# Whole fp32 products in place of three fp32r partial products in a hybrid DeltaNet and attention layer

## The chip, the cores and the metric

The kernel runs on one core of one Trainium2 chip. The metric is the device time of one execution in microseconds. All inputs, outputs and weights are fp32 in device memory.

## The reference

One layer of a diffusion backbone over 2048 latent tokens of width 1024, with 256 context tokens that go through the same weights and only serve as a prefix. A modulated RMS norm gives h; one wide projection of h feeds two token mixers; both are projected to 1024, merged by gates computed from h, projected once more and added to x:

```python
h = _rmsnorm(x, norm_w) * (1.0 + scale[:, None]) + shift[:, None]
...
qkv, beta_r, decay_r, kb, vb = _split_cols(h @ w_state, STATE_SIZES)
za, qb, zb, ga, gb = _split_cols(h @ w_rest, REST_SIZES)
qa, ka, va, g, bt = _gdn_inputs(qkv, beta_r, decay_r, conv_w, a_log, dt_bias)
oa, _, _ = _gdn_bidir(qa, ka, va, g, bt, s_f, s_b, True)
ya = _gdn_output(oa, za, gdn_norm_w)
...
yb = ob * jax.nn.silu(zb)
x = x + gate[:, None] * _merge(ya, yb, ga, gb, w_proj_a, w_proj_b, w_out)
...
def _merge(ya, yb, ga, gb, w_proj_a, w_proj_b, w_out):
    y = jax.nn.sigmoid(ga) * (ya @ w_proj_a) + jax.nn.sigmoid(gb) * (yb @ w_proj_b)
    return y @ w_out
```

The output of attention over window, context and sink is `ob`. The first mixer is a bidirectional gated DeltaNet in chunks of 64 with 4 heads of 128; the second is windowed attention with 8 query heads of 64 on 2 key heads.

## The kernel before

Tokens lie in five groups: gi 0 to 3 of 512 latent tokens, and group 4, the 256 context tokens. Widths are cut into blocks of 128, so a dense product is a loop over k of 8 (over 1024) or 4 (over 512) matmuls that sum up in one PSUM bank of 128 x 512.

**How a dense product is made.** TensorE has an fp32 matmul and a reduced one, fp32r. The kernel uses the reduced one with two parts for each operand: the high part is a copy rounded to fp32r, the low part the fp32 value less the high part. Each step over k is then three fp32r matmuls into the same bank: high by high, low by high, high by low (`fm_dense`, L586 to L588; `tm_dense`, L413 to L415; `project`, L1293 to L1295; `product`, L1556 to L1558). The parts are made by three engines: `make_h` writes h twice, `hh` and `hl`, of the transposed and normed x (ScalarE scales it into `h32`, GpSimd copies the high part, VectorE subtracts, L373 to L376); `weights` loads a column block of w_in into `wr` and splits it into `wh` and `wl` (L239 to L244).

**Stages**, in order of time:
1. Modulation (`mps`, L313): two rows per vector of shift and scale, then the columns `modA` and `modB`.
2. h and the state columns, two token blocks at a time: norm, transpose (`hps`, L371), h, and the 272 narrow columns of w_in (`tmps`, `tm_dense`), from which come the attention keys and values and the decay inputs.
3. q, k and v of the DeltaNet (`qkv`, `lps`): 12 column blocks over all groups, the short convolution on VectorE (L625), norms, transposes and spills to device memory; beside it the decays, and the attention queries (`q_pass`, 256 columns a time).
4. The gates (`gates`, `rest_run`, `rps`): 24 column blocks, first over groups 2 and 3, beside triangular inverses on VectorE (`base`, L809 and L811); then over groups 1 and 0, between the products of the scan.
5. The scan over chunks in both directions (`scan`: `ksps`, `vps`, `sps`, `aps`, `ops`, whole fp32 products of 128 x 128 for each head).
6. Attention (`scores`, `weighted`), with the rest of the gates and the projections of groups 1, 2 and 0 between (`project`, `pps`), let in a few at a time by `paced`.
7. The projections of group 3, and then the output.

**The output stage** multiplies the merged rows `ysp` by w_out, gated by columns. It cuts the 2048 rows into eight units of 256 and w_out into four quarters of 512 x 512 (`B11` to `B22`). Unit 0 takes the eight plain products of quarters; units 1 to 7 take Winograd's form of Strassen's scheme, seven products of quarters each, for which sums of quarters are made (`S1` to `S4` of the rows, `T1` to `T4` of w_out) and every one split into high and low parts. VectorE, ScalarE and GpSimd follow an order written by hand there (`manual_schedule`). The projections of group 3 put off their last two sums (`late_sum`) into that stage.

Elsewhere the order of the instructions on each engine comes from a scheduler that runs over the program with priorities (`high_priority`) and with waits that the program states (`issue_after`). Buffers come from pools; a tile that takes over another's place waits until that one is no longer read.

Of the kernel before, what the change touches and what calls it, by code (L numbers as in the profile page):

```python
# [7 lines left out]
F32 = mybir.dt.float32  # L8
# [32 lines left out]
def _hybrid(ctx, tc, nc, V, S, G, T, ins, out, dbg, upto):  # L41
# [73 lines left out]
    def hpool(name, groups):  # L115
# [9 lines left out]
    hh, hl = {}, {}  # L125
# [27 lines left out]
    def hsrc(c):  # L153

        if c < NCB:
            return hh[4][:, :, c * 128:c * 128 + 128], hl[4][:, :, c * 128:c * 128 + 128]
        b = c - NCB
        o = (b % 4) * 128
        return hh[b // 4][:, :, o:o + 128], hl[b // 4][:, :, o:o + 128]
# [73 lines left out]
    def weights(src, kt, by_act=False):  # L233

        wh = wq.tile([128, KT, 128], F32R, name="wh")
        wl = wq.tile([128, KT, 128], F32R, name="wl")
        for k in range(0, kt, 4):
            wr = wq.tile([128, 4, 128], F32, name="wr", bufs=2)
            dma(wr, src[k * 128:(k + 4) * 128].rearrange("(k p) c -> p k c", p=128))  # L239
            if by_act:  # L240
                S.copy(wh[:, k:k + 4], wr)
            else:
                G.tensor_scalar(wh[:, k:k + 4], wr, 1.0, 1.0, op0=ALU.mult, op1=ALU.mult)  # L243
            V.tensor_tensor(wl[:, k:k + 4], wr, f32(wh[:, k:k + 4]), op=ALU.subtract)  # L244
        return wh, wl
# [4 lines left out]
    if True:  # L250
# [113 lines left out]
        def make_h(xts, hi, lo, cc):  # L364
            n = len(xts) * 128
            for k in range(0, KT, 2):
                h32 = px.tile([128, 2, 256], F32, name="h32", bufs=2)
# [7 lines left out]
                hi_ = G.tensor_scalar(hi[:, k:k + 2], h32[:, :, :n], 1.0, 1.0, op0=ALU.mult, op1=ALU.mult)  # L375
                lo_ = V.tensor_tensor(lo[:, k:k + 2], h32[:, :, :n], f32(hi[:, k:k + 2]), op=ALU.subtract)  # L376
                if k == 2:
                    made = [h, lo_]
# [1303 lines left out]
```

## Time and profile before

| | |
|---|---|
| time, median of 3 runs | 1964.41 us (1963.11 to 1968.98) |
| the profiled execution's own time | 1973.82 us |
| its span | 1972.1 us |
| instructions | 32045 |
| TensorE busy | 1910.1 us, 97% |
| VectorE, ScalarE, GpSimd busy | 1477.4, 815.9 and 657.4 us |
| granted clock of TensorE, mean | 0.991 |

In the profile PE is TensorE's matmuls and PEld its weight loads, DVE is VectorE, ACT ScalarE, POOL GpSimd and SP the engine whose queue issues most transfers; L586 is line 586 of the kernel. A group of instructions has its line, engine, operation, the names of output and inputs, the tile's size, a count, and then busy us and mean ns of one, and the idle time of the engine ahead of it with what ended that. Matmuls are pipelined: the duration of one reaches into the next, so the time that one takes up is read from the distance between two starts. In the timeline a row stands for one or several instructions of a kind (x2): start, length of all, engine, line, names.

### The profile page before, as it was taken

The numbers are of one execution on the slowest core, as the hardware profiler recorded it, in microseconds if no ns is written. First come the engines' busy times: TensorE is split into PE (matmuls) and PEld (weight loads), VectorE is DVE, ScalarE is ACT, GpSimd is POOL, SyncE is SP. The second block draws the span as 40 slices with busy tenths as digits, with TensorE's granted clock in tenths as the row PEclk, the third lists the DMA queues.
The fourth block names the chain that finished last, engine by engine and source line by source line (L and its number), as shares of the span: only waits on it lengthen the run. The fifth ranks groups of instructions, "written<-read, shape, count | busy, mean of one in ns | idle before, by whom it ended". The sixth has DMA issues, their size and how long they took to land. (4 is left out here: it accounts for less than half of the span.)

```text
span 1972.1 us, 32045 instructions
## 1 busy us (share of the span) xinstructions
PE 1910.1 (97%) x10943; PEld 1606.0 (81%) x10943; DVE 1477.4 (75%) x2853; ACT 815.9 (41%) x2008; POOL 657.4 (33%) x750
## 2 busy tenths in 40 slices
PE   6899999989999999999999999999999999999999
PEld 3888888778998787887888888888878887878787
DVE  7889766677776999999778767544787777757864
ACT  6865545554444322211122233324675555532321
POOL 2652111235543201104222334422555444430353
PEclk9999999999999999999999999999999999999999
DMA  7553226765546633537887777755555555448362
GB/s 267 162 154 94 86 89 160 188 163 168 155 149 162 188 106 115 152 93 211 226 243 224 225 217 228 205 157 183 173 164 168 172 164 171 137 120 283 123 224 86
DMA packets 385463, 333.12 MB, mean 169 GB/s; under 512 B 83800, under 2 KB 307344, under 8 KB 384660
## 3 DMA queue, kind: packets, MB, share of 16 engines
q1 hardware_dynamic: 366292, 295.40, 51.7%
q10 hardware_dynamic: 19008, 35.67, 4.9%
q8 instruction: 87, 1.43, 0.3%
q14 instruction: 76, 0.62, 0.1%
HBM read 220.28 MB, written 109.13 MB: 167 GB/s over the span
## 5 line engine op out<-in xcount | busy, mean ns | idle before, releaser
L586 PE MATMUL rps<-hh,wh 128*128 128x512 f32 x768 | 309.8, 403 | 4.3 <-DVE rt L880 3.2
L587 PE MATMUL rps<-hl,wh 128*128 128x512 f32 x768 | 308.3, 401 | 0.0
L588 PE MATMUL rps<-hh,wl 128*128 128x512 f32 x768 | 307.2, 400 | 0.0
L625 DVE SCALAR_TENSOR_TENSOR cacc<-y,cw,cacc 128x512 f32<-128x512 f32 (+1 forms) x224 | 165.0, 758 | 21.1 <-ACT cacc L623 18.8
L586 PEld LDWEIGHTS rps<-hh,wh 128*128 128x128 f32 x768 | 145.4, 189 | 39.8 <-DVE rt L880 3.7
L588 PE MATMUL lps<-hh,wl 128*128 128x512 f32 (+1 forms) x448 | 171.7, 383 | 1.2 <-DVE wl L244 1.2
L586 PE MATMUL lps<-hh,wh 128*128 128x512 f32 (+1 forms) x448 | 172.0, 384 | 0.8 <-POOL wh L243 0.6
L588 PEld LDWEIGHTS rps<-hh,wl 128*128 128x128 f32 x768 | 145.3, 189 | 32.7
L587 PEld LDWEIGHTS rps<-hl,wh 128*128 128x128 f32 x768 | 145.7, 190 | 31.8
L587 PE MATMUL lps<-hl,wh 128*128 128x512 f32 (+1 forms) x448 | 171.0, 382 | 0.0
L1006 DVE TENSOR_TENSOR pl<-pt,ph 128x512 fp32r<-128x512 f32 x156 | 105.5, 685 | 45.8 <-ACT ph L1004 44.9
L1004 ACT CAST ph<-pt 128x512 fp32r<-128x512 f32 x156 | 90.6, 585 | 110.7 <-PE pt L1002 72.1
L878 ACT ACTIVATE rt<-rps 128x512 f32<-128x512 f32 x96 | 57.2, 596 | 185.1 <-PE rps L588 168.2
L978 DVE CUSTOM_DVE_ANT_0 pr<-sc,band,sk 128x640 f32<-128x640 f32 (+1 forms) x128 | 106.7, 862 | 19.9 <-PE sc L974 12.7
L811 DVE TENSOR_TENSOR N<-N,btmp 128x62 f32<-128x62 f32 (+30 forms) x124 | 118.1, 953 | 3.0
L988 POOL TENSOR_SCALAR pr<-pr,sm 128x640 f32<-128x640 f32 (+1 forms) x128 | 101.0, 809 | 55.8 <-DVE sm L986 40.3
L809 DVE TENSOR_TENSOR btmp<-N 128x62 f32<-128x62 f32 (+30 forms) x124 | 115.8, 934 | 3.1
L980 ACT ACTIVATE pr<-pr,sm 128x640 f32<-128x640 f32 (+1 forms) x128 | 104.0, 815 | 24.6 <-DVE sm L978 20.9
L244 DVE TENSOR_TENSOR wl<-wr,wh 128x512 fp32r<-128x512 f32 x120 | 90.8, 768 | 24.1 <-POOL wh L243 21.2
L1293 PE MATMUL pps<-yh,wph 128*128 128x512 f32 x256 | 105.7, 415 | 2.1 <-DVE tb L1304 2.0
L243 POOL TENSOR_SCALAR wh<-wr 128x512 fp32r<-128x512 f32 x72 | 50.3, 711 | 159.4 <-PE lps L587 57.2
L1295 PE MATMUL pps<-yh,wpl 128*128 128x512 f32 x256 | 101.9, 399 | 1.2 <-POOL wpl L1255 1.2
(396 smaller groups left out, 4961.4 us busy)
## 6 DMA issues: line engine op xcount, KB each, us to landing
wr<-in_w_in_dram SPq DMA_DIRECT2D x120, 256.0 KB
kw<-Ksp SPq DMA_DIRECT2D x28, 384.0 KB
x<-vsp SPq DMA_DIRECT2D x36, 256.0 KB
k<-ksp SPq DMA_DIRECT2D x34, 256.0 KB
kT<-kTsp SPq DMA_DIRECT2D x34, 256.0 KB
wm<-in_w_mod_dram SPq DMA_DIRECT2D x16, 512.0 KB
xt<-in_x_dram SPq DMA_DIRECT2D x16, 512.0 KB
dtl<-Dsp SPq DMA_DIRECT2D x32, 256.0 KB
```

The source lines that it names most:

```text
L586: T.matmul(ps, lhsT=wh[:, k], rhs=xh[:, k], start=k == 0, stop=False)
L587: T.matmul(ps, lhsT=wh[:, k], rhs=xl[:, k], start=False, stop=False)
L588: T.matmul(ps, lhsT=wl[:, k], rhs=xh[:, k], start=False, stop=k == kt - 1)
L625: V.scalar_tensor_tensor(a, y[:, t:t + n], cw[:, m, t:t + 1], a, op0=ALU.mult, op1=ALU.add)
L809: V.tensor_tensor(tv, A[:, m + 1:, m].unsqueeze(2).to_broadcast([h1 + n, r, m]), A[:, m, 0:m].unsqueeze(1).to_broadcast([h1 + n, r, m]), o ...
L811: V.tensor_tensor(A[:, m + 1:, 0:m], A[:, m + 1:, 0:m], tv, op=ALU.add)
L978: V.tensor_tensor_reduce(s_, ps[:, o:768], band[:, b0:b0 + W + 256], -0.125, sk[:, 1, hd:hd + 1], ALU.add, ALU.min, sm[:, h, 1:2])
L980: S.activation(s_, s_, AF.Exp, scale=-1.0, bias=sm[:, h, 1:2], accum_out=sm[:, h, 2:3])
L988: G.tensor_scalar(p[:, h, :W + 256], p[:, h, :W + 256], sm[:, h, 3:4], 1.0, op0=ALU.mult, op1=ALU.mult)
L1006: V.tensor_tensor(pl, pt, f32(ph), op=ALU.subtract)
L1293: T.matmul(ps, lhsT=wh[:, k, ms], rhs=hs[k], start=k == 0, stop=False)
L1295: T.matmul(ps, lhsT=wl[:, k, ms], rhs=hs[k], start=False, stop=k == 3)
```

## The change

All dense products but those of attention become whole fp32 products: one matmul for each step over k, of operands that are not split. h is kept once, as fp32, and written half by ScalarE and half by VectorE. Weights are loaded into the buffer that is multiplied from. The two projections load their 512 x 1024 weights whole. The output stage has no units and no quarters: w_out is loaded in eight rows of blocks, multiplied by the gate, and every block of 128 rows takes 2 x 8 plain products; no sums are put off. Attention, the scan, the inverses and the modulation keep their products. The core of the diff:

```diff
-            hh[gi] = p_.tile([128, KT, n], F32R, name=f"hh{gi}", tag=f"hh{gi}")
-            hl[gi] = p_.tile([128, KT, n], F32R, name=f"hl{gi}", tag=f"hl{gi}")
+            hh[gi] = p_.tile([128, KT, n], F32, name=f"hh{gi}", tag=f"hh{gi}")
...
-    def weights(src, kt, by_act=False):
-
-        wh = wq.tile([128, KT, 128], F32R, name="wh")
-        wl = wq.tile([128, KT, 128], F32R, name="wl")
-        for k in range(0, kt, 4):
-            wr = wq.tile([128, 4, 128], F32, name="wr", bufs=2)
-            dma(wr, src[k * 128:(k + 4) * 128].rearrange("(k p) c -> p k c", p=128))
-            if by_act:
-                S.copy(wh[:, k:k + 4], wr)
-            else:
-                G.tensor_scalar(wh[:, k:k + 4], wr, 1.0, 1.0, op0=ALU.mult, op1=ALU.mult)
-            V.tensor_tensor(wl[:, k:k + 4], wr, f32(wh[:, k:k + 4]), op=ALU.subtract)
-        return wh, wl
+    def weights(src):
+
+        w = wq.tile([128, KT, 128], F32, name="wh")
+        for k in range(0, KT, 4):
+            dma(w[:, k:k + 4], src[k * 128:(k + 4) * 128].rearrange("(k p) c -> p k c", p=128))
+        return w
...
-                for i in range(2):
-                    h = S.activation(h32[:, i, :n], ps[:, i, :n], AF.Identity, scale=modA[:, k + i, cc:cc + 1],
-                                     bias=modB[:, k + i, cc:cc + 1])
-                hi_ = G.tensor_scalar(hi[:, k:k + 2], h32[:, :, :n], 1.0, 1.0, op0=ALU.mult, op1=ALU.mult)
-                lo_ = V.tensor_tensor(lo[:, k:k + 2], h32[:, :, :n], f32(hi[:, k:k + 2]), op=ALU.subtract)
+                a, b = (m[:, k:k + 2, cc:cc + 1] for m in (modA, modB))
+                h = S.activation(ht[:, k], ps[:, 0, :n], AF.Identity, scale=a[:, 0], bias=b[:, 0])
+                v = V.tensor_scalar(ht[:, k + 1], ps[:, 1, :n], a[:, 1], b[:, 1], op0=ALU.mult, op1=ALU.add)
...
-                T.matmul(ps[:, :n], lhsT=xh[:, k], rhs=wh[:, k], start=k == 0, stop=False)
-                T.matmul(ps[:, :n], lhsT=xl[:, k], rhs=wh[:, k], start=False, stop=False)
-                T.matmul(ps[:, :n], lhsT=xh[:, k], rhs=wl[:, k], start=False, stop=k == KT - 1)
+                T.matmul(ps[:, :n], lhsT=xh[:, k], rhs=w[:, k], start=k == 0, stop=k == KT - 1)
...
-    def fm_dense(ps, w, xh, xl, kt=KT, behind=(-1, -1)):
-        wh, wl = w
-        for k in range(kt):
-            with paced(behind[2 * k // kt]):
-                T.matmul(ps, lhsT=wh[:, k], rhs=xh[:, k], start=k == 0, stop=False)
-                T.matmul(ps, lhsT=wh[:, k], rhs=xl[:, k], start=False, stop=False)
-                T.matmul(ps, lhsT=wl[:, k], rhs=xh[:, k], start=False, stop=k == kt - 1)
+    def fm_dense(ps, w, x, behind=(-1, -1)):
+        for k in range(KT):
+            with paced(behind[2 * k // KT]):
+                T.matmul(ps, lhsT=w[:, k], rhs=x[:, k], start=k == 0, stop=k == KT - 1)
...
                     for k in range(4):
-                        T.matmul(ps, lhsT=wh[:, k, ms], rhs=hs[k], start=k == 0, stop=False)
-                        T.matmul(ps, lhsT=wh[:, k, ms], rhs=ls[k], start=False, stop=False)
-                        T.matmul(ps, lhsT=wl[:, k, ms], rhs=hs[k], start=False, stop=k == 3)
+                        T.matmul(ps, lhsT=wp[j][:, k, ms], rhs=yy[j][k], start=k == 0, stop=k == 3)
...
+        for a, nm in enumerate(("w_proj_a", "w_proj_b")):
+            wp[a] = pj.tile([128, 4, D], F32, name=f"wp{a}", bufs=1)
+            dma(wp[a], ins[nm][0].rearrange("(k p) c -> p k c", p=128))
...
+        gbc = el.tile([128, D], F32, name="gbc")
+        wo = [po.tile([128, 4, D], F32, name=f"wo{i}") for i, po in enumerate((el, er))]
+        with tc.high_priority(tc.cur_priority - p_last):
+            adma(gbc, gsp.to_broadcast([128, D]))
+            for k in range(KT):
+                w = wo[k // 4][:, k % 4]
+                adma(w, ins["w_out"][0, k * 128:k * 128 + 128])
+                V.tensor_tensor(w, w, gbc, op=ALU.mult)
+        for gi in (1, 2, 0, 3):
+            for o in range(4):
+                y = er.tile([128, KT, 128], F32, name="yo", bufs=4)
+                dma(y, ysp[gi][o])
+                rows = slice(gi * 512 + o * 128, gi * 512 + o * 128 + 128)
+                xr = el.tile([128, D], F32, name="xr", bufs=4)
+                dma(xr, ins["x"][0, rows])
+                for c in range(2):
+                    cs_ = slice(c * 512, c * 512 + 512)
+                    ps = acc([128, 512], name="P")
+                    for k in range(KT):
+                        T.matmul(ps, lhsT=y[:, k], rhs=wo[k // 4][:, k % 4, cs_], start=k == 0, stop=k == KT - 1)
+                    V.tensor_tensor(xr[:, cs_], ps, xr[:, cs_], op=ALU.add)
+                    dma(out[0, rows, cs_], xr[:, cs_])
```

The whole of the old output stage (L1372 to L1637), `late_sum`, `split_w` and `proj_w` are removed.

Two places show how the queues stand. The first is TensorE's queue in one step of the scan, before, from behind a state product (`ksps`) to the next one (`vps`); `rps` is the gates' output, `hh`, `hl`, `wh` and `wl` are the high and low parts of h and of the weights:

```order
L586 MATMUL rps<-hh_148,wh 128x512
L587 MATMUL rps<-hl_149,wh 128x512
L588 MATMUL rps<-hh_148,wl 128x512
L586 MATMUL rps<-hh_148,wh 128x512
L587 MATMUL rps<-hl_149,wh 128x512
L588 MATMUL rps<-hh_148,wl 128x512
L586 MATMUL rps<-hh_146,wh 128x512
L587 MATMUL rps<-hl_147,wh 128x512
L588 MATMUL rps<-hh_146,wl 128x512
L586 MATMUL rps<-hh_146,wh 128x512
L587 MATMUL rps<-hl_147,wh 128x512
L1160 MATMUL vps<-x_11285,mw 128x128 x4
```

and the same place now, from the state product on (`mtp` is a transpose, `aps` the old state's output):

```order
L1124 MATMUL ksps<-S_8325,kT_8473 128x128 x3
L562 MATMUL rps<-hh_146,wh 128x512 x5
L1130 MATMUL vps<-x_8432,mw 128x128 x4
L1042 MATMUL mtp<-ident,mx_8506 128x128 x2
L1166 MATMUL aps<-S_8149,qT_8399 128x128 x4
```

Eleven fp32r products between the two state products have become five whole fp32 ones.

The second is VectorE's queue where the output stage begins, before: quarters of w_out (`B`) are multiplied by the gate (kept in `B22h`'s place) and split, and rows of `ysp` (`yA`) are split, between the last sums of the projections (`ta`, `tb`):

```order
L1402 TENSOR_TENSOR B_19430<-B_19430,B22h 128x2048
L1304 SCALAR_TENSOR_TENSOR tb<-tb,pps 128x512 x2
L1309 TENSOR_TENSOR ta<-ta,tb 128x512 x2
L1452 TENSOR_TENSOR B11l<-B_19430,B11h 128x2048
L1437 TENSOR_TENSOR al<-yA_19443,ah 128x512
L1437 TENSOR_TENSOR al<-yA_19445,ah 128x512
L1402 TENSOR_TENSOR B_19431<-B_19431,B22h 128x2048
L1304 SCALAR_TENSOR_TENSOR tb<-tb,pps 128x512 x2
```

and now (`wo` is w_out, `gbc` the gate's row):

```order
L1246 SCALAR_TENSOR_TENSOR ta<-ta,pps 128x512
L1295 TENSOR_TENSOR wo_14947<-wo_14947,gbc 128x1024 x4
L1295 TENSOR_TENSOR wo_14946<-wo_14946,gbc 128x1024
L1246 SCALAR_TENSOR_TENSOR ta<-ta,pps 128x512
L1295 TENSOR_TENSOR wo_14946<-wo_14946,gbc 128x1024 x2
L1246 SCALAR_TENSOR_TENSOR tb<-tb,pps 128x512
L1295 TENSOR_TENSOR wo_14946<-wo_14946,gbc 128x1024
```

The splits are gone, and the eight gatings stand close together, ahead of most of group 3's sums.

More of the change, by code (lines that the diff above doesn't have):

```diff
@@ L551, in _hybrid @@
             c = NCB + gi * 2
-            state_pair(c, [tm_dense(c + j, wh, wl, NST, bank(c + j)) for j in range(2)])
-        first_w = weights(w_in[:, ORDER[0] * 128:ORDER[0] * 128 + 128], KT)
+            state_pair(c, [tm_dense(c + j, wst, NST, bank(c + j)) for j in range(2)])
+        first_w = weights(w_in[:, ORDER[0] * 128:ORDER[0] * 128 + 128])
         pw_.__exit__(None, None, None)
@@ L875, in rest_run @@
         ps = acc([128, 512], name="rps")
-        fm_dense(ps, w, hh[gi], hl[gi], behind=behind)
+        fm_dense(ps, w, hh[gi], behind=behind)
         t = ev.tile([128, 512], F32, name="rt", bufs=2)
@@ L890, in _hybrid, with gates @@
     psum_phase("right", mg0=1, mg1=1, og=1, gd0=1, gd1=1)
-    def gates(ms, gis, beside=(), by_act=False):
+    def gates(ms, gis, beside=()):
         beside = iter(beside)
-        job = rest(ev, ms[0], by_act)
+        job = rest(ev, ms[0])
         for i, m in enumerate(ms):
@@ L910, in _hybrid @@
     with tc.tile_pool(name="gate", bufs=1, reuse_waits="tile") as gp:
-        gates(list(range(24)), (2, 3), behind(4, mod_gate(gp, ones)), by_act=True)
+        gates(list(range(24)), (2, 3), behind(4, mod_gate(gp, ones)))
     LAST = (LAT(14, 15), LAT(0, 1))
@@ L1244, in _hybrid, with load_y, project @@
     bs2_.__exit__(None, None, None)
-    def w_piece(a, j, k):
-        return ins[("w_proj_a", "w_proj_b")[a]][0, k * 128:k * 128 + 128, j * 512:j * 512 + 512]
-    def split_w(a, j, k, wr, eng):
-        wh, wl = wp[a]
-        cs_ = slice(j * 512, j * 512 + 512)
-        S.copy(wh[:, k, cs_], wr)
-        eng.tensor_tensor(wl[:, k, cs_], wr, f32(wh[:, k, cs_]), op=ALU.subtract)
-    def proj_w(a, j):
-        for k in range(4):
-            wr = wq.tile([128, 512], F32, name="wpr", tag="wr", bufs=2)
-            dma(wr, w_piece(a, j, k))
-            split_w(a, j, k, wr, G)
-    def load_y(pool, gi, parts=((0, 0), (0, 1), (1, 0), (1, 1)), yy=None):
-        yy = yy or [([], []), ([], [])]
-        for b, kk in parts:
-            src, po, tags = ((yasp, wq, ("wh", "wl")), (ybsp, pool, ("ybh", "ybl")))[b]
-            yh = po.tile([128, 2, 512], F32R, name="yh", tag=tags[0])
-            yl = po.tile([128, 2, 512], F32R, name="yl", tag=tags[1])
-            for k in range(2 * kk, 2 * kk + 2):
-                yr = wq.tile([128, 512], F32, name="yr", tag="wr", bufs=2)
-                dma(yr, src[gi][k])
-                last["yh", k] = S.copy(yh[:, k % 2], yr)
-                last["yl", k] = V.tensor_tensor(yl[:, k % 2], yr, f32(yh[:, k % 2]), op=ALU.subtract)
-                yy[b][0].append(yh[:, k % 2])
-                yy[b][1].append(yl[:, k % 2])
-        return yy
-    def project(pool, wp, gi, yy=None, first=-99, late=()):
-        yy = yy or load_y(pool, gi)
-        left = []
+    def load_y(pool, gi):
+        yy = [[], []]
+        for b in range(2):
+            src, po, tags = ((yasp, wq, ("wh", "wl")), (ybsp, pool, ("ybh", "ybl")))[b]
+            for kk in range(2):
+                y = po.tile([128, 2, 512], F32, name="y", tag=tags[kk], bufs=2)
+                for k in range(2):
+                    dma(y[:, k], src[gi][2 * kk + k])
+                    yy[b].append(y[:, k])
+        return yy
+    def project(pool, wp, gi, first=-99):
+        yy = load_y(pool, gi)
         for m in range(KT):
@@ new lines, in _hybrid @@
+    with tc.tile_pool(name="p4e", bufs=1, side="right", reuse_waits="tile") as er, \
+            tc.tile_pool(name="p4l", bufs=1, reuse_waits="tile") as el:
+        gbc = el.tile([128, D], F32, name="gbc")
[20 more added lines that the diff above has]
+                    dma(out[0, rows, cs_], xr[:, cs_])
```

357 lines of the change are left out of this document (35 added, 322 removed), and 3 rows, old and new, of the table OPS.

## Prediction

> **What bounds the kernel now.** I read the page's head and its slices first. TensorE is busy 97% of the span, at 90% or more in all but three of the 40 slices, and its granted clock is full.
>
> ```profile
> PE 1910.1 (97%) x10943; PEld 1606.0 (81%) x10943; DVE 1477.4 (75%) x2853; ACT 815.9 (41%) x2008; POOL 657.4 (33%) x750
> PE   6899999989999999999999999999999999999999
> PEclk9999999999999999999999999999999999999999
> ```
>
> An average hides stages, so next the table by stage (length, then busy us of PE, weight loads, VectorE, ScalarE, GpSimd, the clock, DMA share and GB/s). The stages are: modulation; h and the state columns; q, k, v; gates beside the triangular inverses; the scan; attention with the first projections; the last projections; the output.
>
> ```profile
> 0.00:40.00 40.00, 26.81 (x111) 11.24 (x111) 26.92 (x47) 24.70 (x37) 5.39 (x13) 0.96 0.80 299
> 40.00:125.00 85.00, 75.02 (x576) 70.51 (x575) 73.85 (x190) 67.19 (x177) 56.44 (x72) 0.98 0.47 151
> 125.00:620.00 495.00, 483.06 (x2913) 419.10 (x2913) 368.90 (x782) 246.04 (x699) 153.83 (x169) 1.00 0.51 142
> 620.00:900.00 280.00, 276.76 (x1187) 220.98 (x1186) 253.16 (x304) 67.45 (x128) 39.75 (x34) 0.99 0.48 133
> 900.00:1330.00 430.00, 422.93 (x3027) 366.56 (x3026) 302.04 (x711) 111.54 (x366) 142.69 (x220) 0.99 0.77 218
> 1330.00:1745.00 415.00, 404.95 (x2179) 339.76 (x2178) 301.17 (x643) 239.21 (x518) 189.37 (x200) 0.99 0.53 163
> 1745.00:1800.00 55.00, 53.05 (x240) 42.60 (x240) 30.68 (x39) 14.76 (x21) 6.79 (x5) 1.00 0.66 216
> 1800.00:1972.00 172.00, 167.52 (x724) 135.30 (x722) 120.73 (x145) 45.03 (x64) 63.13 (x41) 1.00 0.48 162
> ```
>
> Length less PE busy gives TensorE's idle time: 13.2, 10.0, 11.9, 3.2, 7.1, 10.1, 2.0 and 4.5 us, together 62. So from 40 us on TensorE bounds every stage, and no more than 62 - 13.2 = 48.8 us can be won by shorter waits alone (the first stage is not changed).
>
> Busy does not yet give a price, because a matmul's 0.40 us overlaps the next one. The price is the distance from start to start, in the timeline (start, us, engine, line). Matmuls first, then one weight load:
>
> ```profile
> 700.05 0.39 PE L586 MATMUL rps<-hh,wh 128*128 128x512 f32 x1
> ...
> 703.55 0.39 PE L586 MATMUL rps<-hh,wh 128*128 128x512 f32 x1
> ```
> ```profile
> 700.05 0.19 PEld L587 LDWEIGHTS rps<-hl,wh 128*128 128x128 f32 x1
> ```
>
> The second row is 15 matmuls after the first: 3.50 / 15 = 0.233 us each. The weights of the next one are loaded meanwhile. One step over k is three fp32r products now: 0.700 us.
>
> **The change: the dense steps.** Each three become one whole fp32 product. Counts, from the groups kept apart by shape (the high-high row stands for its two sisters of the same count):
>
> ```profile
> L586 PE MATMUL rps<-hh,wh 128*128 128x512 f32 x768 | 309.8, 403 | 4.3 <-DVE rt L880 3.2 <-ACT rt L878 1.0
> L586 PE MATMUL lps<-hh,wh 128*128 128x512 f32 x384 | 153.4, 399 | 0.2 <-ACT y L696 0.2
> L1293 PE MATMUL pps<-yh,wph 128*128 128x512 f32 x256 | 105.7, 415 | 2.1 <-DVE tb L1304 2.0
> L413 PE MATMUL tmps<-qwh,hh 128*128 128x256 f32 x256 | 72.5, 283 | 1.7 <-ACT y L696 1.7
> L586 PE MATMUL lps<-hh,wh 128*128 128x256 f32 x64 | 18.6, 291 | 0.6 <-POOL wh L243 0.6
> L414 PE MATMUL tmps<-wh,hl 128*128 128x272 f32 x144 | 44.3, 314 | 5.1 <-DVE hl L376 5.0
> L1556 PE MATMUL P<-T3h,ah 128*128 128x512 f32 x28 | 11.1, 395 | 0.0
> L1556 PE MATMUL Pq<-B22h,ah 128*128 128x512 f32 x8 | 3.2, 397 | 0.0
> L313 PE MATMUL mps<-wm,silz 128*4 128x512 f32 x4 | 1.9, 592 | 0.0
> L1160 PE MATMUL vps<-x,mw 128*128 128x128 f32 x144 | 19.1, 275 | 0.0
> ```
>
> No fp32 product of 512 columns with 128 stationary columns is in the trace. The nearest rows are fp32 with 4 stationary columns and 512 moving ones (line 313), and with 128 and 128 (line 1160); the timeline gives their spacing, with an fp32r pair and the narrower fp32r products beside it:
>
> ```profile
> 27.79 0.63 PE L313 MATMUL mps<-wml,sil 128*4 128x512 f32 x2
> 28.35 1.88 PE L313 MATMUL mps<-wm,silz 128*4 128x512 f32 x4
> ```
> ```profile
> 1004.91 1.05 PE L1160 MATMUL vps<-x,mw 128*128 128x128 f32 x8
> ```
> ```profile
> 502.79 0.28 PE L413 MATMUL tmps<-qwh,hh 128*128 128x256 f32 x1
> ...
> 503.95 0.28 PE L414 MATMUL tmps<-qwh,hl 128*128 128x256 f32 x1
> ```
> ```profile
> 80.50 0.29 PE L415 MATMUL tmps<-wl,hh 128*128 128x272 f32 x1
> ...
> 81.50 0.29 PE L415 MATMUL tmps<-wl,hh 128*128 128x272 f32 x1
> ```
>
> Line 313 issues two fp32 products here and line 1160 four (one a head), so each fp32 product leaves two records. Spacing of a record: (1.88 - 0.592) / 3 = 0.429 us at 512 columns; (1.05 - 0.275) / 7 = 0.111 us at 128. A whole product at 512 thus costs 2 x 0.429 = 0.858 us, or, scaled from the full-width rows, 2 x 4 x 0.111 = 0.886. I take 0.858, the row with the same columns; nothing makes it cheaper with more stationary columns. By a line between 0.111 and 0.429, a record is 0.217 at 256 columns and 0.230 at 272. The fp32r steps are 3 x 0.116 = 0.348 (ten steps in 1.16 us) and 3 x 0.125 = 0.375 (eight in 1.00).
>
> One rule speaks against hiding the loads. The Trainium skill ("TensorE: Matmul & The Clock Gate", section "The mechanism" of its Part 3) says a weight load runs beside matmuls only where the row groups differ (elsewhere it also allows a load into a background buffer); its section "LDWEIGHTS (loading the stationary operand)" gives 128 / 1.2 = 107 ns, so an estimate by that page adds 2 x 0.107 to each of 1664 wide products, 356 us more. The trace disagrees: with full 128x128 loads the fp32 records of line 1160 come every 0.111 us, load included.
>
> The sum on TensorE:
> - 768 + 384 + 256 = 1408 wide steps x (0.858 - 0.700): +222.5 us
> - 256 + 64 steps of 256 columns x (0.434 - 0.348): +27.5 us
> - 144 steps of 272 columns x (0.460 - 0.375): +12.2 us
> - output: now seven groups of 28 and four of 8, 228 steps x 0.700 = 159.6 us; after, 16 row tiles x 2 halves x 8 = 256 x 0.858 = 219.6 us: +60.0 us
>
> Together +322 us.
>
> **The splits.** The copies, subtractions and sums of parts on VectorE, ScalarE and GpSimd go. They lie beside TensorE, so they are worth only the waits that they end last. The table of waits (total us, times, longest) has these:
>
> ```profile
> PE tmps L414 <- DVE hl L376: 5.0, 8, 1.3
> PE tmps L413 <- POOL hh L375: 1.2, 3, 0.6
> PE lps L588 <- DVE wl L244: 1.2, 2, 0.8
> PE pps L1295 <- POOL wpl L1255: 1.2, 1, 1.2
> PE P L1558 <- DVE al L1437: 0.8, 1, 0.8
> PE lps L586 <- POOL wh L243: 0.6, 1, 0.6
> ```
>
> That is 10.0 us off. h is written once, half of it by ScalarE and half by VectorE, both idle part of that stage. Weights now land in the buffer that is multiplied from; the next column block is still asked for one block ahead, under 2 x 8 x 0.858 = 13.7 us of gates, so I cost this at nothing; without that cover a load would be exposed once a block. The two 2 MB loads of the projection weights stand in the DMA queue of SP before attention starts, a stage ahead of their use.
>
> **The scan** needs other work between its dependent products. In the rows of TensorE's queue shown with the change, 11 gate records (rps) stand between two state products (ksps, then vps) before, 11 x 0.233 = 2.6 us; now five whole products do, 5 x 0.858 = 4.3 us. The same steps are issued in all, with more cover in each gap. Of the scan's and attention's 17.2 us of idle I take 8 off.
>
> **The output's start.** By the rows of VectorE's queue shown there, all eight gatings of w_out stand ahead of most of group 3's sums (ta, tb). Half of w_out and the gate's row (2.6 MB) are asked for on ScalarE's queue after its last attention copy; the sums queued behind the gating wait for them, and TensorE's PSUM banks for the sums. Eight banks hold 8 x 4 x 0.858 = 27 us of projections. At the 216 GB/s of that stage 2.6 MB take 12 us, at half of it 24; the gating itself, 2.29 us for 128x2048 before
>
> ```profile
> 1780.93 2.29 DVE L1402 TENSOR_TENSOR B<-B,B22h 128x2048 f32<-128x2048 f32 x1 [4.96 <-DMA B22h<-gsp]
> ```
>
> is 8 x 1.15 = 9 us, partly behind the loads. I take nothing; if the cover fails, about 10 us. The output begins with row group 1, whose sums are stored long before, so the last sums, no longer put off, hold up nothing.
>
> **The rivals.**
> - Dearer records. An fp32r record takes 0.233 us, while half an fp32 record at 512 is 0.215. If full-width streaming were the cause, fp32 would take 2 x 0.233 = 0.466: 1664 x 2 x 0.037 = +123 us, 2391 us. Against it: the fp32r pair with only 4 stationary columns (0.63 us for both, less 0.39 for one) is 0.24 apart too, right beside the fp32 ones. Chance 0.07.
> - More cover. All 62 us of idle go, not 18: 2224 us. But the first 13.2 are untouched and long attention chains stay. 0.04.
> - Not slower: the two records of a product overlap where many stand in a row, which two lone products can't show. All dense work is 1310 us now; in records it is 3806 of 512 columns (narrower ones in proportion), so it breaks even at 0.344 us a record. At fp32r's 0.233 it would be 887 us, and the kernel 1964 - 18 - 424 = 1522 us, just above VectorE's 1477. The Trainium skill (same page, "Back-to-back issue gap") states 131 ns a matmul of 512 columns in real streams, by which a product would cost 0.262; the trace's streams show 0.233 for one record. Against: line 1160's eight records in a row show no overlap (0.111 against 0.429 / 4 = 0.107). Chance 0.02.
>
> **How the numbers follow.** The profiled execution took 1973.8 us around a span of 1972.1, 9.4 above the median of 1964.4. It becomes 1973.8 + 322 - 10 - 8 = 2278; the median 2268. Upper end: 0.886 a product adds 1664 x 0.028 = 47, a failed cover 10: 2325, rounded to 2330. Lower end: all 48.8 us of waits go instead of 18: 2237, to 2230 for gaps too short to count as idle. The forecast has 0.85, 0.02 falls between it and the dearer records. About 0.3% is what a measurement here can tell from no change: faster 0.015, the same 0.01, slower 0.975.
>
> **What would show it.** Right: two records a product, 0.43 us apart, in the gates; the gates' stage of 48 groups near 48 x 8 x 0.858 = 329 us; the output near 220 us; PE idle around 45. Wrong: records at 0.37 or less, or 0.46; a gap of over 10 us before the first output product; PE idle above 70.

## The result, and the profile after

The changed kernel takes 2278.81 us (median of 4 runs, 2278.03 to 2285.34), the kernel before 1966.07 us beside it (4 runs): a ratio of 1.1598, 95% interval 1.1569 to 1.1627. The profiled execution took 2285.34 us around a span of 2283.6, and the mean granted clock is 0.991 as before.

The first lines of the page after: busy time of each engine, and TensorE in 40 slices.

```profile
PE 2225.8 (97%) x8899; PEld 1321.4 (58%) x8899; DVE 1254.6 (55%) x2586; ACT 705.7 (31%) x1804; POOL 475.4 (21%) x575
...
PE   7999999999999999999999999998999999999999
```

TensorE has 19% fewer records and 315.7 us more busy time; VectorE lost 222.8 us, ScalarE 110 and GpSimd 182, and the kernel is slower by nearly what TensorE gained (the span grew by 311.5 us). Next the costliest groups kept apart by shape, then two pieces of the timeline of after: records in the gates, and the first ones after an idle piece.

```profile
L562 PE MATMUL rps<-hh,wh 128*128 128x512 f32 x1536 | 686.2, 600 | 15.5 <-DMA wh<-in_w_in_dram 9.3 <-DVE rt L850 6.0 <-ACT rt L848 0.2
L1240 PE MATMUL pps<-y,wp 128*128 128x512 f32 x512 | 229.2, 594 | 4.3 <-DMA y<-ybsp 3.6 <-DVE ta L1246 0.7
L1307 PE MATMUL P<-wo,yo 128*128 128x512 f32 x512 | 219.9, 592 | 0.0
```
```profile
719.48 8.75 PE L562 MATMUL rps<-hh,wh 128*128 128x512 f32 x20
...
744.91 2.07 PE L562 MATMUL rps<-hh,wh 128*128 128x512 f32 x2 [5.95 <-DVE rt L850]
```

Each product leaves two records (1536 for 768 steps). Twenty of them take (8.75 - 0.600) / 19 = 0.429 us each, the number that the prediction took from a row with 4 stationary columns. Behind a long idle piece they are dearer: 2.07 us for two, with a granted clock of 0.50 from 744 to 750 us. The output stage has no wait at all (0.0).

The table of stages, cut at each kernel's own boundaries, compares the two (length, then busy us of PE, weight loads, VectorE, ScalarE, GpSimd, the clock, DMA share, GB/s). Before, from h and the state columns to the output:

```profile
40.00:129.00 89.00, 78.42 (x602) 73.61 (x600) 76.75 (x199) 69.54 (x186) 58.91 (x75) 0.98 0.49 156
129.00:615.50 486.50, 475.16 (x2866) 412.35 (x2867) 362.44 (x765) 242.79 (x688) 149.00 (x163) 1.00 0.50 140
615.50:936.00 320.50, 315.83 (x1407) 252.51 (x1406) 291.46 (x353) 73.31 (x140) 59.41 (x53) 0.98 0.53 147
936.00:1330.00 394.00, 388.36 (x2826) 338.67 (x2825) 267.30 (x669) 106.59 (x356) 125.40 (x203) 0.99 0.76 215
1330.00:1762.00 432.00, 421.95 (x2264) 353.42 (x2262) 310.35 (x656) 244.82 (x527) 193.25 (x203) 0.99 0.53 162
1762.00:1809.00 47.00, 45.05 (x193) 36.15 (x193) 29.32 (x34) 14.12 (x15) 2.92 (x2) 1.00 0.71 237
1809.00:1972.00 163.00, 158.52 (x685) 128.09 (x683) 112.91 (x136) 40.05 (x60) 63.13 (x41) 1.00 0.47 160
```

The same stages after:

```profile
40.00:131.00 91.00, 84.96 (x456) 71.01 (x455) 59.89 (x195) 55.07 (x150) 29.49 (x39) 0.98 0.47 155
131.00:694.00 563.00, 559.58 (x2159) 350.49 (x2158) 333.09 (x723) 244.84 (x685) 120.49 (x132) 1.00 0.42 120
694.00:1076.00 382.00, 367.37 (x932) 165.82 (x930) 263.38 (x312) 47.90 (x92) 54.20 (x52) 0.98 0.47 126
1076.00:1560.00 484.00, 477.91 (x2687) 309.88 (x2687) 235.20 (x621) 112.19 (x363) 99.42 (x161) 0.99 0.61 179
1560.00:2005.00 445.00, 433.55 (x1920) 290.52 (x1919) 288.88 (x621) 221.73 (x481) 167.73 (x183) 0.99 0.52 161
2005.00:2060.00 55.00, 55.00 (x129) 24.39 (x129) 24.55 (x31) 0.58 (x1) 2.35 (x2) 1.00 0.64 203
2060.00:2283.60 223.60, 219.74 (x513) 96.94 (x511) 23.46 (x34) 0.00 (x0) 0.00 (x0) 1.00 0.28 95
```

| stage | busy of TensorE, measured | price on record | idle before | idle after |
|---|---|---|---|---|
| h and state columns | +6.5 | +12.2 | 10.6 | 6.0 |
| q, k, v | +84.4 | +60.7 + 27.5 = +88.2 | 11.3 | 3.4 |
| gates to last projections | +162.6 | 1024 x 0.158 = +161.8 | 22.3 | 32.2 |
| output | +61.2 | +60.0 | 4.5 | 3.9 |

Idle is length less busy, from one traced execution of each kernel, so differences of a few us are no more than hints; in the third row the gates' stage alone went from 4.7 to 14.6. With the first stage (13.2 and 12.3) it comes to 62.0 before and 57.8 after, where the prediction had taken off 18 and expected about 45. The waits of after that are new say where (total us, times, longest):

```profile
PE rps L562 <- DMA wh<-in_w_in_dram: 9.3, 3, 5.6
PE rps L562 <- DVE rt L850: 6.0, 1, 6.0
PE sc L941 <- DMA qT<-Qsp: 4.2, 1, 4.2
PE pps L1240 <- DMA y<-ybsp: 3.6, 1, 3.6
PE tmps L393 <- ACT hh L365: 3.2, 6, 1.4
```

The waits for hl, wl, wpl and al have gone. In their place TensorE waits in the gates for a block of weights and for VectorE, and at the seam of scan and attention for a load of the query.

### The profile page after: what moved, and what is told of

It is laid out like the page before. It is cut to its first block, busy times and chain, and to the rows that moved or that the text cites. A ratio compares the mean times of both kernels' runs of the same rounds, so it can differ in the third digit from the quotient of the medians.

```text
span 2283.6 us, 26933 instructions
## 1 busy us (share of the span) xinstructions
PE 2225.8 (97%) x8899; PEld 1321.4 (58%) x8899; DVE 1254.6 (55%) x2586; ACT 705.7 (31%) x1804; POOL 475.4 (21%) x575
## 4 chain that ended last, share of the span: by engine, by line
PE 87%; DMA 6%; DVE 3%; ACT 2%; SPq 1%; issue 1%; POOL 0%; DVEq 0%; ACTq 0%; POOLq 0%
PE rps L562 26%; PE lps L562 15%; PE P L1307 10%; PE pps L1240 9%; PE tmps L393 6%; PE pt L972 3%; PE av L979 2%; PE av L978 1%; PE ksps L1124 1%; PE sps L1142 1%; PE ops L1177 1%; PE aps L1166 1%; PE vps L1130 1%; PE sc L941 1%; PE gps L640 1%; DMA wh<-in_w_in_dram 1%
## 5 line engine op out<-in xcount | busy, mean ns | idle before, releaser
L562 PE MATMUL rps<-hh,wh 128*128 128x512 f32 x1536 | 686.2, 600 | 15.5 <-DMA wh<-in_w_in_dram 9.3
L562 PEld LDWEIGHTS rps<-hh,wh 128*128 128x128 f32 x1536 | 287.1, 192 | 345.3 <-issue 330.9
L562 PE MATMUL lps<-hh,wh 128*128 128x512 f32 (+1 forms) x896 | 373.8, 563 | 0.5 <-ACT y L670 0.5
L562 PEld LDWEIGHTS lps<-hh,wh 128*128 128x128 f32 x896 | 166.2, 190 | 152.0 <-issue 145.2
L1240 PE MATMUL pps<-y,wp 128*128 128x512 f32 x512 | 229.2, 594 | 4.3 <-DMA y<-ybsp 3.6
L1307 PE MATMUL P<-wo,yo 128*128 128x512 f32 x512 | 219.9, 592 | 0.0
L1307 PEld LDWEIGHTS P<-wo,yo 128*128 128x128 f32 x512 | 97.3, 190 | 122.5 <-issue 122.5
L393 PE MATMUL tmps<-qwh,hh 128*128 128x256 f32 x512 | 119.8, 386 | 0.4 <-ACT y L670 0.3
L393 PEld LDWEIGHTS tmps<-qwh,hh 128*128 128x128 f32 x512 | 96.2, 192 | 17.8 <-issue 5.3
L972 PE MATMUL pt<-ident,pr 128*128 128x128 f32 x624 | 93.6, 273 | 0.0
```

The costliest lines, as they stand in the source:

```text
L393: T.matmul(ps[:, :n], lhsT=xh[:, k], rhs=w[:, k], start=k == 0, stop=k == KT - 1)
L562: T.matmul(ps, lhsT=w[:, k], rhs=x[:, k], start=k == 0, stop=k == KT - 1)
L972: T.transpose(pt[:, h], p[:, h, kb * 128:kb * 128 + 128], ident)
L1240: T.matmul(ps, lhsT=wp[j][:, k, ms], rhs=yy[j][k], start=k == 0, stop=k == 3)
L1307: T.matmul(ps, lhsT=y[:, k], rhs=wo[k // 4][:, k % 4, cs_], start=k == 0, stop=k == KT - 1)
```

## The experiments

**One part alone: the output stage.** The kernel before, with the output stage of the change.

```diff
-        sums67 = project(pj, wp, 3, late=(6, 7))
+        project(pj, wp, 3)
...
+                        T.matmul(ps, lhsT=y[:, k], rhs=wo[k // 4][:, k % 4, cs_], start=k == 0, stop=k == KT - 1)
```

> The kernel before with the output stage of the change alone: plain whole fp32 products, no quarters, no put-off sums; all other products keep three fp32r parts. Theory (TensorE's time is records times their spacing, everywhere): the output goes from 228 steps x 0.700 = 160 us to 256 x 0.858 = 220 us, so +60 us, 2026 us in all. Rival (the order written by hand and the put-off sums hid waits that come back): +70 us or more, with TensorE idle for over 10 us before the first output product.

Measured: 2039.1 us (4 runs), ratio 1.037 (1.0345 to 1.0395), 74 us more than before. The group of output products in its trace:

```profile
L1395 PE MATMUL P<-wo,yo 128*128 128x512 f32 x512 | 221.7, 596 | 4.2 <-DMA yo<-ysp 4.2
```

The stage has its price (221.7 against 219.6 worked out). Ahead of its first product stands a wait of 4.2 us for a row tile. It is no gap of over 10 us, so the rival's mechanism is not seen, though the total lies on its side. Of the 14 us beyond the price, 2 are the stage and 4.2 the wait. The two traces are alike up to there (the last projection starts at 1808.8 us before and at 1808.6 here), and the two profiled executions lie 66.5 us apart (2040.34 and 1973.82), which is the price with these two. The other 7.6 us come with the medians: the profiled execution of the kernel before was 8.9 us longer than its median beside this run (1964.93). The tiles of w_out and x also take other buffers here than in the whole change, so the wait need not be one that the change could have.

**The same stage with fp32r products.** As above, but each step is three fp32r products, of row tiles that ScalarE first copies to fp32r.

```diff
+                        for x in range(3):
+                            T.matmul(ps, lhsT=yh[:, k], rhs=wo[k // 4][:, k % 4, cs_], start=k == 0 and x == 0,
+                                     stop=k == KT - 1 and x == 2)
```

> The kernel before with a plain output stage in which every step is three fp32r products, no sums of quarters. The low parts are left out: the product of the high parts is issued three times, so only the time is meant. Theory: 256 steps x 0.700 = 179 us against 160, +20 us, 1986 us; the other 40 of the 60 us belong to the fp32 product itself. Rival (the sums of quarters cost in waits what they save in products): no change, or faster.

Measured: 1994.83 us, ratio 1.0148 (1.0124 to 1.0172), 30 us more than before. Its output group:

```profile
L1399 PE MATMUL P<-wo,yoh 128*128 128x512 f32 x768 | 178.5, 395 | 6.8 <-ACT yoh L1390 5.9 <-DVE wo L1384 1.0
```

256 x 0.700 = 179.2 was the price, and 178.5 is the busy time. Between the two runs lie 44 us, and 256 x 0.158 = 40. So the output's loss has two parts: some 20 us for giving up the seven-product scheme (179 against 160) and some 40 for fp32. By the medians 10 to 14 us come on top in each run, by the profiled executions (1996.51 and 2040.34, less 1973.82) only 2.7 and 6.5. The waits at the start show 6.8 and 4.2; the whole change does not pay them, its output group has no wait.

**The splits kept.** The kernel before with whole fp32 products of the high parts and the plain output; all splits are still made.

```diff
-                T.matmul(ps, lhsT=wh[:, k], rhs=xh[:, k], start=k == 0, stop=False)
-                T.matmul(ps, lhsT=wh[:, k], rhs=xl[:, k], start=False, stop=False)
-                T.matmul(ps, lhsT=wl[:, k], rhs=xh[:, k], start=False, stop=k == kt - 1)
+                T.matmul(ps, lhsT=f32(wh[:, k]), rhs=f32(xh[:, k]), start=k == 0, stop=k == kt - 1)
```

> The kernel before with the plain fp32 output and with one whole fp32 product for each dense step, but h, the weights and the projections' inputs are still split into high and low parts; the low parts go unused (the products take the high parts alone, so the result is coarser). Theory (the splits lie beside TensorE): 1966 + 322 = 2288 us, 5 to 18 above the change's 2279. Rival (the splits load memory, VectorE and GpSimd so that TensorE waits for them, and their removal gave much back): over 2310.

Measured: 2314.18 us, ratio 1.1774 (1.1756 to 1.1792), 35 us above the change by the medians, 25.8 between the two profiled executions (2311.15 and 2285.34). That is past the theory's 5 to 18 us and on the rival's side. Not all of it belongs to the splits, though: the output stage here is that of the first experiment, which cost more than its price. The longest waits:

```profile
PE sc L967 <- DMA qT<-Qsp: 11.6, 1, 11.6
PE hps L371 <- ACT h L373: 8.6, 5, 3.7
```

With the splits TensorE waits 8.6 us in the stage of h, for ScalarE's scaling, and q, k, v begin at 140.6 us, against 131.2 after the change. The wait at the seam before attention, 11.6 against 4.2, is for a load, and a run below has 11.4 there without any splits; gates and scan together are only 2.4 us longer than after the change (706.4 to 1587.7, against 694.2 to 1573.1). Of the 25.8 us, 9.4 lie in h, 2.8 in q, k, v, 2.4 in gates and scan, 8.3 from there to the output, of which 4.0 are a wait for the output's first row tile, and 2.8 in the output itself. Without the 6.8 us at the output some 19 us are left (by the medians 21, which is 35 less the 14 of the first experiment). So the splits were worth about twice the 10 us that the prediction had for them, as much as its 18 for splits and cover together. Only in h does the trace show a wait for one of the splitting engines; where the rest comes from was not tried by itself.

**The wait for a block of weights: other loads ahead of it.** In the changed kernel, loads of w_mod stand ahead of the block's load in SP's queue near 738. This run gives them four buffers in place of two.

```diff
-                wm = pool.tile([128, 512], F32, name="wmg", bufs=2)
+                wm = pool.tile([128, 512], F32, name="wmg", bufs=4)
```

> The changed kernel with four buffers in place of two for the rows of w_mod that the gate's sum reads beside the first gates. Theory (the changed kernel's new waits of TensorE for weights, 9.3 us, come from weight loads that stand in SP's queue behind a w_mod load that waits for its buffer): the longest of them, 5.6 us and the slow clock after it, goes: 2279 - 8 = 2271. Rival (the load itself is late, or too close to its use): no change.

Measured: 2276.91 us, ratio 1.1585 (1.1567 to 1.1602), 2 us below the change, with intervals of the two ratios that overlap. The wait for the block is longer, 13.6 us in five pieces. The longest, 7.2 us, stands at 738, where the trace of after has the 5.95 us that were put down to VectorE's step on rt. The block's own longest wait after the change stands at 871:

```profile
876.91 5.49 PE L562 MATMUL rps<-hh,wh 128*128 128x512 f32 x9 [5.62 <-DMA wh<-in_w_in_dram]
```

That one fell to 2.3 us in this run. The block's load near 738 went out hardly sooner with the added buffers, at 736.13 in place of 737.96. So the theory that these loads hold it fell. The windows around that place in this run (PE busy second, the last three columns clock, DMA share, GB/s):

```profile
710.00:720.00 10.00, 10.00 (x24) 4.40 (x24) 3.02 (x4) 1.39 (x3) 0.00 (x0) 1.00 1.07 182
730.00:740.00 10.00, 8.32 (x20) 3.42 (x18) 8.85 (x11) 1.21 (x2) 3.39 (x3) 1.00 0.97 209
740.00:750.00 10.00, 4.46 (x6) 1.92 (x7) 8.49 (x9) 3.33 (x5) 5.51 (x4) 0.53 0.78 222
```

The transfer engines are full (1.07, 0.97) ahead of the idle piece: the inputs of the triangular inverses and rows of w_mod are loaded there. And behind the idle piece the clock is granted at 0.53.

**The blocks asked for earlier.** The changed kernel with three buffers for a block and two blocks of lead.

```diff
-        job = rest(ev, ms[0])
+        jobs = [rest(ev, m) for m in ms[:2]]
         for i, m in enumerate(ms):
...
-                    nxt = rest(ev, ms[i + 1]) if i + 1 < len(ms) else None
+                    if i + 2 < len(ms):
+                        jobs.append(rest(ev, ms[i + 2]))
```

> The changed kernel with three buffers for a column block of w_in in place of two, and in the gates every block asked for two blocks ahead in place of one (27 us of products ahead instead of 14). My theory now: the three waits for a block, 9.3 us in all, come from loads that start on time and are slow, because the inverses' loads of 1 MB fill the transfer engines; with twice the lead they go, and with them the 7 us in which the clock is halved after the longest two: 9.3 less, and some 5 less, about 2265 us. The rival: the block's load is issued late, because it stands in SP's queue behind a transfer that itself waits (the query of the inverses' inputs), and asking earlier in the program changes little: waits for a block stay above 5 us and the time stays within 5 us of 2279.

Measured: 2289.84 us, ratio 1.1631 (1.1607 to 1.1656): slower than the change by 11 us by the medians, which neither theory had, and by 6.5 by the two ratios, whose intervals overlap. The 14 us that the theory promised are not there in either case. Its longest waits:

```profile
PE sc L941 <- DMA qT<-Qsp: 11.4, 1, 11.4
PE rps L562 <- DVE rt L850: 7.4, 1, 7.4
```

The waits for a block are gone, as the theory said. But near 743 an idle piece stands as before, put down to VectorE's step on rt: VectorE's queue waits for the inverse's input, and rt's step is queued behind. And the seam before attention went from 4.2 to 11.4 us; in this run no gate product stands between the scan's last products and attention, where after the change 32 of their records do. Another 4.0 us are lost ahead of the gates (q, k, v begin at 135.2 us in place of 131.2). Two waits stood at one place, and taking one away showed the other.

**The blocks' loads left out.** The changed kernel, where all blocks of the gates' first half are multiplied with the first one.

```diff
+        w = w or weights(w_in[:, col + mm * 128:col + mm * 128 + 128])
...
+                    nxt = rest(ev, ms[i + 1], job[0] if len(ms) == 24 else None) if i + 1 < len(ms) else None
```

> The changed kernel with 23 of the 24 loads of a column block in the first half of the gates left out; all blocks there are multiplied with the first one. It asks what the waits near 738 and 871 come from (9.3 us put down to the block's load, 6.0 to VectorE's step on rt). My theory after the runs with more buffers: near 738 VectorE's queue waits for the 1 MB loads of the second inverse (3 us and 3 us idle at N), its steps on rt stand behind, and TensorE's banks stay full, so over 4 us of the wait there stay; only the one at 871, where the block's load stands behind a 2 MB store, goes: 6 to 8 us less, about 2272 us. The rival, that the loads of the blocks themselves are the cause of both: both waits go, and with the half clock behind them 15 us or more less, 2264 us or under.

Measured: 2268.6 us (5 runs), ratio 1.1525 (1.1502 to 1.1547), 10 below the change (14 by the two ratios), between the two numbers. The waits decide for the theory:

```profile
PE rps L562 <- DVE rt L850: 4.4, 1, 4.4
...
PE rps L562 <- DMA wh<-in_w_in_dram: 2.2, 2, 1.9
```

The idle piece at 738 is still there (4.4 us, on rt), the one at 871 has gone. The loads of the blocks are worth 10 to 14 us in the change, and the idle piece that is left at 738 goes with the input of the inverses. Leaving the loads out also takes them off the transfer engines, so the run does not say whether a block's lateness or its share of the transfers costs these us.

**The seam before attention.** The changed kernel with one store on another queue.

```diff
-            dma(yasp[b // 4][:, :, b % 4 * 128:b % 4 * 128 + 128].rearrange("h p t -> p h t"), sza)
+            adma(yasp[b // 4][:, :, b % 4 * 128:b % 4 * 128 + 128].rearrange("h p t -> p h t"), sza)
```

> The changed kernel with one edit: the store of the scan's rows (yasp from sza) is issued on ScalarE's queue in place of SP's. In the trace of the changed kernel the first loads of attention stand behind the scan's last such store in SP's queue; it goes out at 1562.3, when its row is ready, and the query load at 1566.4, and TensorE waits 4.2 us for that load at 1568 and then runs 6.8 us at half clock. My theory, that this order is the cause of the wait at the seam of scan and attention: the loads are issued some 7 us earlier, the wait and most of the half clock go, 4 to 8 us less, about 2273 us, and attention starts before 1569. The rival, that the loads are held by the buffers that they take over from the scan: the wait stays over 3 us, the time within 2 us of 2279.

Measured: 2276.58 us, ratio 1.1566 (1.1546 to 1.1585), 2 us below the change by the medians; the intervals of the two ratios overlap, so the time alone decides nothing. The scan's last products and the loads in SP's queue, after the change and then in this run:

```profile
1553.08 1.05 PE L1177 MATMUL ops<-v,qd 128*128 128x128 f32 x8
```
```profile
1562.32 0.36 SPq L1095 DMA_DIRECT2D yasp<-sza  x1
...
1566.35 0.43 SPq L923 DMA_DIRECT2D qT<-Qsp  x1
```
```profile
1545.14 1.05 PE L1177 MATMUL ops<-v,qd 128*128 128x128 f32 x8
```
```profile
1553.65 2.39 SPq L906 DMA_DIRECT2D band<-in_k_mats_dram  x3
1558.76 0.33 SPq L909 DMA_DIRECT2D sk<-in_sink_dram  x1
1559.66 0.33 SPq L923 DMA_DIRECT2D qT<-Qsp  x1
```

From the scan's last products to the query's load it is 13.3 us after the change and 14.5 in this run: taking the store away did not bring the load forward. The queue goes on sooner (`band` at 8.5 us) and then stops again ahead of `sk`. TensorE's wait is 2.5 us in place of 4.2: from the load's issue to the first product of attention it is 3.8 us here (1563.5) and 6.7 after the change (1573.1). So the theory of the store's order falls; that the loads wait for buffers, the rival, fits the second stop, but it was not tried by itself.

**What other time is left: fewer products in the gates.** The kernel before, with two products a step in the gates, and then with one.

```diff
-        fm_dense(ps, w, hh[gi], hl[gi], behind=behind)
+        fm_dense(ps, w, hh[gi], hl[gi], behind=behind, low=False)
...
+                if low:
+                    T.matmul(ps, lhsT=wh[:, k], rhs=xl[:, k], start=False, stop=False)
+                    T.matmul(ps, lhsT=wl[:, k], rhs=xh[:, k], start=False, stop=k == kt - 1)
```

With two products only the first of these two stands under the condition.

> The kernel before, with the gates' products cut from three fp32r products a step to two; the product of the high part of the weights and the low part of h is left out there, 768 matmuls, and nothing else is changed. My theory, that TensorE's records alone set the time of the gates, the scan and attention, and that idle stays as it was: 768 x 0.233 = 179 us less, about 1786 us. The rival, that part of the price in these stages is paid by cover (the scan's and attention's chains need so many products between them, and VectorE is busy 70% of the gates' stage): TensorE's idle from the gates to the projections grows by over 20 us, and the time is above 1806 us.

> The kernel before, with the gates' products cut from three fp32r products a step to one, high by high; the other two, 1536 matmuls of 0.233 us or 358 us, are left out there. Cut to two it took 1930 us, 38 less where 179 were taken away, and the BF16 parts gave 25 of 76. Gates and scan together lasted 726 us before, and 708 in both of those runs. My theory now: something else than TensorE's records, the chains of the inverses and of the scan over VectorE and the transfers, sets a floor just under the time of before there, so a further cut of 179 us returns under 30 us: 1900 to 1935 us, and gates and scan stay between 660 and 715 us. The rival, that two products left a bad order with long idle pieces, and no floor: a further cut returns over 60 us, under 1870 us.

Measured: 1930.0 us with two products (ratio 0.9804, 0.9778 to 0.983) and 1946.27 with one (0.9889, 0.9868 to 0.9909). So of 179 us of records 38 came back, and of 358 only 22. The rival of the first run holds: TensorE's idle time from the gates to the last projections went from 22 us to 121. The floor of the second run's theory holds too, though its time even rose by 16 us, 11 past the theory's range. The gates' stage and the scan with one product:

```profile
615.90:913.00 297.10, 213.06 (x862) 152.03 (x860) 245.44 (x327) 97.64 (x178) 90.96 (x87) 0.90 0.79 224
913.00:1341.90 428.90, 253.75 (x2042) 228.99 (x2040) 310.66 (x704) 90.33 (x325) 111.35 (x174) 0.76 0.60 168
```

Together 726 us, as long as in the kernel before, and 11 past the theory's 715, with TensorE busy 467 us of it and the clock down at 0.90 and 0.76. With two products these stages take 708 us. Up to the first `vps` product of the scan it is 244 us with two products and 288 with one, from there to attention 464 and 438; why the first part grew was not tried. The longest idle piece, in TensorE's timeline, and VectorE's at the end of it:

```profile
1083.29 1.09 PE L1073 MATMUL mtp<-ident,mx 128*128 128x128 f32 x4 [48.39 <-DMA mx<-Xsp]
```
```profile
1068.88 0.29 DVE L812 TENSOR_TENSOR N<-N,btmp 128x122 f32<-128x122 f32 x1
```

The scan waited 48.4 us for a block of the inverse, and VectorE's last steps of that inverse end at 1069.

**Half of the inverse's steps.** To see whether that is the floor: every second step of the two large inverses left out, in the kernel before and in the one with one product.

```diff
-        for m in range(1, 63):
+        for m in range(1, 63, 2):
```

> The kernel before, with every second step of the two large triangular inverses left out (lines 809 and 811: 118.1 + 115.8 = 233.9 us of VectorE, of which half, some 117 us, go). Nothing of TensorE changes. If TensorE bounds the gates and the scan there, as the prediction said, only waits can go: 4 to 15 us less, 1953 to 1964 us. The rival, that the inverses are a bound of their own already in the kernel before: 30 us or more less, under 1938 us.

> The gates with one product a step (high by high, as in the run of that kind, 1946 us), and with every second step of the two large inverses left out as well. My theory, that the floor found there is the chain of the inverses on VectorE: TensorE waited 48.4 us for a block of the inverse at 1034 while VectorE still worked on it until 1069. With some 117 us of VectorE gone that wait goes, and the run returns 60 us or more against 1946: under 1886 us. The rival, that the transfers, 0.79 busy in the gates' stage there, or the scan's own chain set the floor: under 25 us, over 1921 us.

Measured: the kernel before becomes 1972.42 us (8 runs), ratio 1.0045 (1.0029 to 1.0061), no gain at all; with one product the time falls to 1805.4 us (ratio 0.9199, 0.9182 to 0.9217), 141 us below 1946. The first lines of the two pages:

```profile
PE 1909.2 (97%) x10943; PEld 1601.8 (81%) x10943; DVE 1369.0 (69%) x2729; ACT 818.1 (42%) x2008; POOL 651.8 (33%) x750
```
```profile
PE 1612.2 (89%) x9407; PEld 1351.2 (75%) x9407; DVE 1371.8 (76%) x2729; ACT 820.2 (45%) x2008; POOL 658.6 (37%) x750
```

The kernel before has TensorE's records as its bound: 108 us of VectorE gone, and TensorE's busy time and the span stayed (the 0.45% was not followed up; the profiled spans are 1970.4 and 1972.1). With one product TensorE's wait on `mtp` for blocks of the inverse (mx from Xsp) fell from 58.8 us to 7.6. So the chain of the inverses is a second bound, hardly lower, which shows as soon as records go.

**BF16 parts.** The kernel before, with the parts of h and of the columns of w_in as BF16 tiles.

```diff
-            hh[gi] = p_.tile([128, KT, n], F32R, name=f"hh{gi}", tag=f"hh{gi}")
+            hh[gi] = p_.tile([128, KT, n], BF16, name=f"hh{gi}", tag=f"hh{gi}")
```

> The kernel before, with the high and low parts of h, of the columns of w_in and of the query and state weights kept as BF16 tiles in place of fp32r ones (a coarser result); the projections and the output stage stay fp32r. Counts of matmuls and all else stay. It asks what the 0.233 us of an fp32r record belong to, since half of a whole fp32 product takes 0.2145. If the extra 0.0185 us belong to fp32r: 3 x 1152 products of 512 columns x 0.0185 = 64 us less, the products of 256 and 272 columns 12 us less, together 76 us less, about 1889 us. The rival, that they belong to streams of products with a reload of the weights each time whatever the type: spacing 0.233 stays, and the time stays within 10 us of 1965, or a little under it for cheaper copies and subtractions.

Measured: 1943.34 us, ratio 0.9865 (0.9841 to 0.989), 25 less. The first and last of 24 records in a row in its gates:

```profile
699.87 0.38 PE L587 MATMUL rps<-hl,wh 128*128 128x512 bf16 x1
...
704.83 0.38 PE L586 MATMUL rps<-hh,wh 128*128 128x512 bf16 x1
```

4.96 / 23 = 0.216 us: the extra time does belong to fp32r, as the theory had it. But only a third of the 76 us came back, as with the products left out. Gates and scan took 708 us in place of 726 where 43 us of records had gone. This is the one version here that beats the kernel before with all its products and steps in place, by 1.3% and with a coarser result.

## Why the prediction was right, point by point

**The bound.** That TensorE bounds every stage from 40 us on is right for a change that adds records, and the halved inverses show it. It is no statement about a change that takes records away. The rival of overlapping records put 1522 us down to TensorE alone, "just above VectorE's 1477"; the run with one product a step shows that gates and scan stay near 726 us even with a third of the gates' records.

**The price.** Two records of 0.429 us hold, in the gates and in the output, with full 128 x 128 loads. So dearer records (0.466), overlap (0.344 or less) and the Trainium skill's rule in "TensorE: Matmul & The Clock Gate", section "The mechanism", which by the prediction's estimate made 356 us more, are all out. The first 768 records of the gates keep TensorE busy for about 335 us, where the prediction gave 329 as a sign of being right. Where products stand in long rows, price and measurement agree within 1.2 us (gates to projections, output). In the stages of h and of q, k, v the busy time rose 5.7 and 3.8 us less than priced. The narrow whole products have their price (16 records of 256 columns take 3.62 us, (3.62 - 0.386) / 15 = 0.216 each, where 0.217 was forecast); whether the difference lies in the narrow fp32r steps or in short waits that count as busy stays open.

**The waits: the step that failed.** The prediction took 10 us off for the splits and 8 for more cover in the scan and in attention. Idle time fell by 4.2, to 57.8, between the about 45 given as a sign of being right and the 70 given as a sign of being wrong. Two things were mis-sized, in opposite directions:
- The splits were worth more, about 19 us by the run that kept them, where the trace of before names only 10. Half of the 19 is h, which is late once products are whole and h is still split; the cause of the other half is not shown.
- New waits came. In the gates' stage idle rose by 9.9, most of it at two places where the inverses move 1 to 2 MB: the loads of weight blocks, costed "at nothing" under a cover of 13.7 us, are worth 10 to 14 (blocks left out), and VectorE stands on the inverse's input with rt's step behind it. In the scan and attention more cover gained nothing (idle 15.7 before, 17.5 after): the longest wait there, 4.2 us, is for a load at the seam, which no product between two state products can cover.

**The start of the output.** Taken as nothing, and so it is: the first output product follows 0.4 us behind the last projection, without a wait. In the run with the output stage alone 4.2 us stand there, for a row tile; that is neither the gating nor the loads of w_out that the prediction weighed.

**The sum.** The price was 6.5 us too high and the waits 13.8 too low, which gives 2285.3 for the profiled execution in place of 2278. The step down to the median was 6.5 and not 9.4. These 7.3 and 2.9 us are, but for rounding, the 10.8 us between 2268 and 2278.81. That the total came so near is in part luck: the error of the price took away half of the error of the waits.

## What to carry to other kernels

An engine at 97% says what added work costs, not what removed work gains: look for the chain that ends next (here the inverses on VectorE, which let only 22 of 358 us come back). Price a change of product type by the distance from start to start of records that the trace already has, also where its shape is not quite the same. And count a load as covered only where the transfer engines are free at that time; if a wait is taken away, ask which wait stands behind it at the same place.

## What the runs showed of the hardware

- At 512 columns an fp32r record takes 0.233 us, a BF16 one 0.216, and a whole fp32 product 0.858: fp32r pays 8% over BF16, and fp32 takes as long as four BF16 products (0.864). The Trainium skill ("TensorE: Matmul & The Clock Gate", section "Back-to-back issue gap") gives N / 2.4 + 2.5 ns, 216 at 512 columns, for a matmul by itself and 131 in a stream: the BF16 stream here agrees with the first figure, fp32r and fp32 have prices of their own, and no stream showed the second.
- An idle piece can cost twice. After the 5.95 us at 738 two fp32 records took 2.07 us, at a granted clock of 0.50. In the run with one product a step, where idle pieces are many, the clock was 0.76 over the scan, and 0.925 over the whole run against 0.991 before.
- A wait can be put down to either of two late parties: the idle piece of 4 to 7 us that begins at 738 to 743 was named after VectorE in the change (5.95) and after the block's load in the run with four w_mod buffers (7.2).
